# A two-layer hybrid decoder trunk: three more granules of weights split through GpSimd's DMAs, the last pair of MoBA heads in tiles of its own, and branch B in two phases

## The chip, the cores and the metric

The kernel runs on one core of a Trainium2 chip. The metric is the device time of one execution in microseconds, as the median of several runs. The profile quoted is of one execution of the same program.

## The reference

Two layers, each a gated token mixer and a SwiGLU, both with a residual and a LayerNorm behind. SEQ is 256, D_MODEL 1024, everything float32. What the change touches is the end of the mixer:

```python
def hybrid_mixer(x, w_in, w_branch_sb, w_branch_moba, w_out):
    proj = x @ w_in      # q,k,v of 8 stick-breaking heads, q,k,v of 8 MoBA heads, two gates
    ...
    o_sb = stick_breaking_attention(...)
    o_mb = moba_attention(...)           # 256 keys are one block: causal softmax attention
    branch_sb = merge_heads(o_sb) @ w_branch_sb      # [256,512] @ [512,1024]
    branch_mb = merge_heads(o_mb) @ w_branch_moba    # [256,512] @ [512,1024]
    merged = jax.nn.sigmoid(g_sb) * branch_sb + jax.nn.sigmoid(g_mb) * branch_mb
    return merged @ w_out                            # [256,1024] @ [1024,1024]

# per layer
x = layer_norm(alpha * x + hybrid_mixer(x, ...))
x = layer_norm(alpha * x + (silu(x @ w_gate) * (x @ w_up)) @ w_down)
```

## The kernel before

**Three products for one.** Every float32 operand is split into a rounded part `hi` and the rest `lo` (both in the type fp32r), and a product is three matmuls on TensorE (PE): hi by hi, lo by hi, hi by lo. The helper `mm3` issues them, and `mm` records them, so PE's rows all stand on L427.

**Granules.** The weights of a layer are cut into 122 granules of 128x1024 float32 (512 KB). A ring of 10 slots (`NSPLIT`) holds split granules, `whi` and `wlo`; a slot comes free when PE is done with the granule ten before. There are two ways to split a granule. A *hard* one is loaded by SyncE's queue into one of 6 `raw` buffers, cast to `whi` by ScalarE (ACT, L48), and `wlo` = raw - whi is made by VectorE (DVE, L53). A *soft* one (the numbers in `SOFT_IN_LAYER`) needs neither `raw` nor DVE: a DMA issued by GpSimd (POOL) casts it into `whi` on the way, ACT writes -whi into `wlo` (ACTIVATE, L48), and a second DMA of GpSimd adds the weight to `wlo`. GpSimd issues its DMAs in order, each behind what it waits for. Granules 40 to 47 are moved in a pattern of two pieces (L134), the others in one (L137).

Numbers in a layer: 24 to 39 are the gates (PE tiles `pg`), 40 to 43 branch A, which is the stick-breaking side (`pa0` to `pa3`), 44 to 47 branch B, the MoBA side (`pb0` to `pb3`), 48 to 55 the output projection (`pw`), behind it the SwiGLU. In names, `l0` and `l1` are the layers; layer 1's granules are numbered 122 higher.

**MoBA's pairs.** The eight MoBA heads go in four pairs, `mb0` to `mb3`. A pair's softmax weights are turned on DVE and on a way through DRAM (tiles `turn` and `scr`), split into `pp` (a single buffer with a hi and a lo half), and summed with v on PE (`mb_o`). ACT copies the sums of the hi half into `f`, DVE adds the rest, and `f` is split into one 128-row part of `omb_hi` and `omb_lo`, which is step k = p of branch B's contraction. `bounced` makes each pair wait until the one before has been summed, since they share `pp` (the list `summed`).

**Branch B.** `branch(i, 1, ps, ks)` issues the contraction steps `ks` of output granule i, for each of its two 128-column halves: 6 matmuls a step. Before the change these are the steps 0 and 1 of granules 0 to 2 (36 matmuls), then step 2 of granules 0 to 2 (18) and steps 0 and 1 of granule 3 (12), then the rest. `summed_up` multiplies a finished granule by its gate, adds branch A's share (`gate`), and splits it into `m_hi` and `m_lo`, the operands of `pw`.

**Order.** Each engine runs its instructions in the order in which they are recorded. A planner (`Weave`) sets it as the program is built: generators (`split_line`, `bounced` and others) yield the time at which they can go on, by costs written in the program, and are stepped in between the matmuls; `weave.finish(sides)` records all that is left of the named generators first.

## Time and profile before

| | us |
|---|---|
| median of 3 runs | 725.62 (725.59 to 725.67) |
| the profiled execution | 725.78 |
| its span (first to last instruction) | 724.0 |
| PE busy | 710.8 |
| DVE busy | 528.6 |
| ACT busy | 389.8 |
| POOL busy | 34.5 |

The profile's times start at the beginning of the span; the profiled execution's time lies 1.78 us above its span. The stretch of which the prediction speaks, from the end of the gates to the output projection, lies at about 112 to 175 us in layer 0 and at 467 to 530 us in layer 1. Matmuls are pipelined: a row's duration overlaps the next one's, and what a matmul costs is read from start to start.

### The profile page before, as it was taken

What the parts mean: (1) busy time and instruction counts of PE and PEld (TensorE: products, weight loads), DVE (VectorE), ACT (ScalarE), POOL (GpSimd) and SP (SyncE); (2) the same over time, 40 slices, a digit from 0 to 9 for tenths busy, and PEclk for the clock granted to TensorE, in tenths of its full rate; (3) what the DMA queues carried; (4) which work ended last, traced back from release to release, by engine and by line L of the source; (5) the groups of instructions that cost most, each with busy time, mean ns of one, the idle gap of its engine ahead of it and who ended that gap; (6) DMA issues with size and microseconds to landing.
All of it is one profiled execution on the core that took longest, in us unless ns stands there. A gap on an engine that the chain in (4) does not pass through costs nothing.

```text
span 724.0 us, 12718 instructions
## 1 busy us (share of the span) xinstructions
PE 710.8 (98%) x4984; PEld 650.5 (90%) x4984; DVE 528.6 (73%) x790; ACT 389.8 (54%) x581; POOL 34.5 (5%) x48
## 2 busy tenths in 40 slices
PE   8999999999999999999999999999999999999995
PEld 6889899987899999988889889999788999998885
DVE  5999886798886666643688887869989776665416
ACT  5767667654665554442365566775555555454300
POOL 0001110000000000000000111100010000000001
PEclk9999999999999999999999999999999999999999
DMA  8998889776596655476259589795749965663501
GB/s 294 337 342 234 226 214 270 223 247 234 188 333 220 202 183 196 146 293 200 80 163 353 164 218 232 201 297 175 265 136 290 295 217 180 200 202 99 224 1 58
DMA packets 61596, 156.26 MB, mean 216 GB/s; under 512 B 10720, under 2 KB 21984, under 8 KB 61536
## 3 DMA queue, kind: packets, MB, share of 16 engines
q1 hardware_dynamic: 56848, 140.50, 58.2%
q0 software_dynamic: 4544, 14.68, 9.4%
q8 instruction: 39, 0.64, 0.4%
q10 hardware_dynamic: 144, 0.26, 0.1%
q14 instruction: 21, 0.17, 0.1%
HBM read 148.08 MB, written 7.34 MB: 215 GB/s over the span
## 4 chain that ended last, share of the span: by engine, by line
PE 87%; DVE 7%; DMA 3%; issue 2%; ACT 1%; SPq 0%; POOL 0%; POOLq 0%; DVEq 0%; ACTq 0%
PE l1pf L427 14%; PE l0pf L427 14%; PE l0pd L427 8%; PE l0pg L427 6%; PE l1pg L427 5%; PE l1pe L427 4%; PE l1pd L427 4%; PE l1pft L427 3%; PE l1pqk L427 3%; PE l0pqk L427 3%; PE l0pft L427 3%; PE l1pvq L427 3%; DVE wlo L53 3%; PE l1pw L427 2%; PE l0pw L427 2%; PE l1pk L427 2%
## 5 line engine op out<-in xcount | busy, mean ns | idle before, releaser
L53 DVE TENSOR_TENSOR wlo<-raw,whi 128x1024 fp32r<-128x1024 f32 (+1 forms) x234 | 277.5, 1202 | 83.0 <-ACT whi L48 80.1
L48 ACT CAST whi<-raw 128x1024 fp32r<-128x1024 f32 (+1 forms) x233 | 237.6, 1035 | 83.8 <-PE l0pd L427 19.6
L427 PE MATMUL l1pf<-xT_hi,wlo 128*128 128x256 f32 x288 | 79.6, 276 | 0.0
L427 PE MATMUL l1pf<-xT_hi,whi 128*128 128x256 f32 x288 | 79.6, 276 | 0.0
L427 PE MATMUL l1pf<-xT_lo,whi 128*128 128x256 f32 x288 | 79.6, 276 | 0.0
L427 PE MATMUL l0pf<-xT_hi,wlo 128*128 128x256 f32 x288 | 79.5, 276 | 0.0
L427 PE MATMUL l0pf<-xT_hi,whi 128*128 128x256 f32 x288 | 79.5, 276 | 0.0
L427 PE MATMUL l0pf<-xT_lo,whi 128*128 128x256 f32 x288 | 79.5, 276 | 0.0
L427 PEld LDWEIGHTS l1pf<-xT_hi,whi 128*128 128x128 f32 x288 | 54.1, 188 | 0.0
L427 PEld LDWEIGHTS l1pf<-xT_lo,whi 128*128 128x128 f32 x288 | 54.1, 188 | 0.0
L427 PEld LDWEIGHTS l1pf<-xT_hi,wlo 128*128 128x128 f32 x288 | 54.1, 188 | 0.0
L427 PEld LDWEIGHTS l0pf<-xT_hi,whi 128*128 128x128 f32 x288 | 54.1, 188 | 0.0
L427 PEld LDWEIGHTS l0pf<-xT_lo,whi 128*128 128x128 f32 x288 | 54.1, 188 | 0.0
L427 PEld LDWEIGHTS l0pf<-xT_hi,wlo 128*128 128x128 f32 x288 | 54.1, 188 | 0.0
L427 PE MATMUL l0pg<-xT_hi,whi 128*128 128x256 f32 x128 | 35.8, 280 | 0.2 <-DVE l0vmb L53 0.2
L427 PE MATMUL l1pg<-xT_hi,whi 128*128 128x256 f32 x128 | 35.7, 279 | 0.0
L427 PE MATMUL l0pg<-xT_hi,wlo 128*128 128x256 f32 x128 | 35.4, 277 | 0.0
L427 PE MATMUL l0pg<-xT_lo,whi 128*128 128x256 f32 x128 | 35.4, 276 | 0.0
L427 PE MATMUL l1pg<-xT_lo,whi 128*128 128x256 f32 x128 | 35.4, 276 | 0.0
L427 PE MATMUL l1pg<-xT_hi,wlo 128*128 128x256 f32 x128 | 35.4, 276 | 0.0
L427 PE MATMUL l0pd<-whi,l0h_hi 128*128 128x512 f32 x88 | 34.5, 392 | 0.0
L427 PE MATMUL l0pd<-whi,l0h_lo 128*128 128x512 f32 x88 | 34.3, 389 | 0.0
(349 smaller groups left out, 1783.2 us busy)
## 6 DMA issues: line engine op xcount, KB each, us to landing
raw<-in_w_dram SPq DMA_DIRECT2D x226, 512.0 KB, 4.8
whi<-in_w_dram POOLq DMA_DIRECT2D x14, 512.0 KB, 5.0
wlo<-in_w_dram POOLq DMA_DIRECT2D x14, 512.0 KB, 6.5
ln<-in_ln_dram SPq DMA_DIRECT2D x8, 512.0 KB, 6.1
raw<-in_w_dram SPq DMA_DIRECT2D x7, 256.0 KB, 6.1
l0mb_scr<-l0mb_turn SPq DMA_DIRECT2D x4, 384.0 KB, 4.9
l0mb_turn<-l0mb_scr SPq DMA_DIRECT2D x16, 96.0 KB, 6.1
l1mb_scr<-l1mb_turn SPq DMA_DIRECT2D x4, 384.0 KB, 7.1
```

What stands on the lines that cost most here:

```text
L48: f(*args, **kw)
L53: f(*args, **kw)
L427: nc.tensor.matmul(o, a, b, start=start, stop=stop)
```

## The change

Three edits. (1) Granule 40 of each layer becomes hard and 43, 46, 49 and 52 become soft, so that a layer has 10 soft granules instead of 7. (2) The last pair (p = 3) gets two tiles of its own, `w0` and `w1`, for the hi and the lo of its weights, and does not wait for `summed`; since these are two tiles, its sums are eight matmuls of 256 and 128 columns, where they were four of 512 and 256. Of pairs 2 and 3, `f` now lies in the last 256 columns of the `turn` tile. (3) Branch B runs steps 0 and 1 of all four granules first (48 matmuls), then finishes all pairs, then runs steps 2 and 3 together.

```diff
-SOFT_IN_LAYER = (22, 25, 28, 31, 34, 37, 40)
+SOFT_IN_LAYER = (22, 25, 28, 31, 34, 37, 43, 46, 49, 52)
...
     def bounced(name, p, src, there, v, oT, e, f):
         pT, e = yield from bounce_line(name, there, there, src, 6, e)
-        begun.append(name)
-        ...
-        parts = (blocked(pp[:, i].rearrange("p h (k c) -> p (h k) c", c=P)) for i in range(2))
-        e = yield from split_line(*parts, pT, 768, e)
-        yield from both_parts(name, p, v, oT, e, p == NPAIR - 1)
+        if p == NPAIR - 1:
+            ws = [pl.tile([P, 2, 384], F32R, tag="T", name=f"{name}_w{i}") for i, pl in enumerate((work, page0))]
+        else:
+            begun.append(name)
+            mine = len(begun)
+            while len(summed) < mine:
+                yield
+            e = max(e, summed[-1])
+            yield e
+            ws = [pp[:, i] for i in range(2)]
+        e = yield from split_line(*(blocked(x.rearrange("p h (k c) -> p (h k) c", c=P)) for x in ws), pT, 768, e)
+        yield from both_parts(name, p, v, oT, e, ws if p == NPAIR - 1 else None, f)
...
         for h, o in enumerate(os):
             vs = [x[:, p, 2 * h:2 * h + 2, :].rearrange("p r c -> p (r c)") for x in v]
-            mm(o, vs[0], pp[:, :, h, :S], True, False)
-            mm(o[:, :, P:], vs[1], pp[:, :, h, S:], False, True)
+            if ws:
+                for i, w in enumerate(ws):
+                    mm(o[:, i], vs[0], w[:, h, :S], i == 0, False)
+                    mm(o[:, i, P:], vs[1], w[:, h, S:], False, i == 1)
+            else:
+                mm(o, vs[0], pp[:, :, h, :S], True, False)
+                mm(o[:, :, P:], vs[1], pp[:, :, h, S:], False, True)
         e = pe_done()
-        summed.append(e)
+        if not ws:
+            summed.append(e)
...
-            there = unit(f"{name}_turn", [P, 1024])[:, :768]
+            there = unit(f"{name}_turn", [P, 1024])
+            there, f = there[:, :768], there[:, 768:]
...
-        for i in range(3):
-            branch(i, 1, pbs[i], range(2))
-        weave.finish(sides[:-1])
-        for i in range(3):
-            branch(i, 1, pbs[i], range(2, 3))
-        branch(3, 1, pbs[3], range(2))
+        for i in range(4):
+            branch(i, 1, pbs[i], range(2))
         weave.finish(sides)
...
-        branch(0, 1, pbs[0], range(3, 4))
+        branch(0, 1, pbs[0], range(2, 4))
...
         for i in (1, 2):
-            branch(i, 1, pbs[i], range(3, 4))
+            branch(i, 1, pbs[i], range(2, 4))
```

The order on DVE in layer 0, from the end of branch A to the end of branch B. A number behind a name counts the buffers that the program has taken; for `raw46` to `raw50` the first number is the granule. `wlo_99<-raw..` is the split of a hard granule, `mb2_f` and `mb3_f` the additions of the last two pairs, `omb_lo` their splits. Before:

```order
L53 TENSOR_TENSOR wlo_99<-raw46_1477,whi_98 128x1024
L53 TENSOR_TENSOR l0mb2_f_1729<-l0mb2_o0_1718,l0mb2_f_1729 64x256 x2
L53 TENSOR_TENSOR l0mb2_f_1729<-l0mb2_o1_1719,l0mb2_f_1729 64x256 x2
L53 TENSOR_TENSOR pp_168<-l0mb3_turn_1412,pp_168 128x768
L53 TENSOR_TENSOR l0gate3_1455<-l0gate3_1455,l0pa3_1707 128x2x256
L53 TENSOR_TENSOR wlo_99<-raw47_1491,whi_98 128x1024
L53 TENSOR_TENSOR wlo_99<-raw48_1504,whi_98 128x1024
L53 TENSOR_TENSOR l0omb_lo_1018<-l0mb2_f_1729,l0omb_hi_1017 128x256
L53 TENSOR_TENSOR wlo_99<-raw49_1540,whi_98 128x1024
L53 TENSOR_TENSOR l0mb3_f_1803<-l0mb3_o_1791,l0mb3_f_1803 64x256 x4
L53 TENSOR_TENSOR wlo_99<-raw50_1556,whi_98 128x1024
L53 TENSOR_TENSOR l0omb_lo_1018<-l0mb3_f_1803,l0omb_hi_1017 128x256
```

After, at the same place:

```order
L53 TENSOR_TENSOR l0mb3_w1_1708<-l0mb3_turn_1411,l0mb3_w0_1707 128x768
L53 TENSOR_TENSOR wlo_99<-raw47_1476,whi_98 128x1024
L53 TENSOR_TENSOR l0mb2_turn_1374<-l0mb2_o0_1726,l0mb2_turn_1374 64x256 x2
L53 TENSOR_TENSOR l0mb2_turn_1374<-l0mb2_o1_1727,l0mb2_turn_1374 64x256 x2
L53 TENSOR_TENSOR l0gate3_1453<-l0gate3_1453,l0pa3_1714 128x2x256
L53 TENSOR_TENSOR wlo_99<-raw48_1501,whi_98 128x1024
L53 TENSOR_TENSOR l0mb3_turn_1411<-l0mb3_o_1750,l0mb3_turn_1411 64x256 x4
L53 TENSOR_TENSOR l0omb_lo_1018<-l0mb2_turn_1374,l0omb_hi_1017 128x256
L53 TENSOR_TENSOR wlo_99<-raw50_1515,whi_98 128x1024
L53 TENSOR_TENSOR l0omb_lo_1018<-l0mb3_turn_1411,l0omb_hi_1017 128x256
```

The splits of 46 and 49 are gone from this row, and the last pair's weights (`w1`) are split ahead of pair 2's additions. Behind it come the splits of 51 and 53, and 54 between the additions of the first gate (before: 51 alone). Ahead of the last `m_lo` four splits stood in a row (52 to 55), and now that of 55 alone.

The order on ACT in layer 0, around the split of pair 0's weights (`pp`). Before:

```order
L48 CAST whi_98<-raw39_973 128x1024
L48 CAST whi_98<-raw41_1074 128x1024
L48 CAST whi_98<-raw42_1078 128x1024
L48 CAST pp_168<-l0mb0_turn_1197 128x768
L48 CAST whi_98<-raw43_1146 128x1024
```

After:

```order
L48 CAST whi_98<-raw39_973 128x1024
L48 ACTIVATE wlo_99<-whi_98 128x1024
L48 CAST whi_98<-raw40_1074 128x1024
L48 CAST whi_98<-raw41_1078 128x1024
L48 CAST pp_168<-l0mb0_turn_1197 128x768
L48 ACTIVATE l0gate3_1453<-l0pg6_1454 128x512
L48 CAST whi_98<-raw42_1146 128x1024
```

The ACTIVATE is the negation of granule 43, now ahead of the casts of 40 and 41 and of `pp`; it can start when GpSimd's first DMA of 43 has landed.

The order on GpSimd in layer 0, where the last soft granules are issued, as a difference (- before, + after):

```order
 L137 DMA whi<-in_w_dram 128x1024
 L137 DMA wlo<-in_w_dram 128x1024
-L134 DMA whi<-in_w_dram 128x2x512
-L134 DMA wlo<-in_w_dram 128x2x512
+L134 DMA whi<-in_w_dram 128x2x512 x2
+L134 DMA wlo<-in_w_dram 128x2x512 x2
+L137 DMA whi<-in_w_dram 128x1024 x2
+L137 DMA wlo<-in_w_dram 128x1024 x2
 L58 ISA
```

Granule 40's two DMAs are replaced by those of 43 and 46, both casts first, and behind them those of 49 and 52, before GpSimd's own small work (`ISA`) of the LayerNorm.

## The prediction

> **What bounds the kernel now.** I read the page first, then the waits of TensorE (PE), then PE's timeline around each wait.

> ```profile
> span 724.0 us, 12718 instructions
> PE 710.8 (98%) x4984; PEld 650.5 (90%) x4984; DVE 528.6 (73%) x790; ACT 389.8 (54%) x581; POOL 34.5 (5%) x48
> ...
> PE l0pw L427 <- DVE l0m_lo L53: 0.8, 1, 0.8
> PE l1pw L427 <- DVE wlo L53: 0.7, 2, 0.5
> PE l0pb L427 <- DVE l0omb_lo L53: 0.6, 1, 0.6
> PE l0pw L427 <- DVE wlo L53: 0.4, 1, 0.4
> PE l1pb L427 <- DVE l1omb_lo L53: 0.4, 1, 0.4
> ```

> PE is busy for 98% of the span, and no PE work is taken out, so only its idle time can be won. The waits (total us, times, longest) list six of them in the stretch that the change touches: pb and pw, in both layers, all on VectorE (DVE). They sum to 2.9 us. An idle figure understates the loss, because the matmul after a wait also starts late. PE's timeline (start, duration) shows that:

> ```profile
> 150.07 0.28 PE L427 MATMUL l0pb<-l0omb_hi,whi 128*128 128x256 f32 x1
> 150.98 0.39 PE L427 MATMUL l0pb<-l0omb_lo,whi 128*128 128x256 f32 x1 [0.63 <-DVE l0omb_lo L53]
> 151.20 0.28 PE L427 MATMUL l0pb<-l0omb_hi,wlo 128*128 128x256 f32 x1
> ...
> 160.79 0.50 PE L427 MATMUL l0pw<-wlo,l0m_hi 128*128 128x512 f32 x1 [0.45 <-DVE wlo L53]
> ...
> 164.79 0.50 PE L427 MATMUL l0pw<-whi,l0m_lo 128*128 128x512 f32 x1 [0.77 <-DVE l0m_lo L53]
> ...
> 130.98 0.70 PE l0mb_o L427 x4
> 131.68 7.53 PE l0pa L427 x66
> ```

> The last two rows are from the chain that ended last: 66 matmuls of 256 columns in 7.53 us are 0.114 us each. In the first three, two starts that should take 2 x 0.114 take 1.13: 0.90 is lost where the row says 0.63, so 0.27 more. The six waits lose 2.9 + 6 x 0.27 = 4.5 us, 2.6 of it in layer 0. That is the most the change can win.

> **Why DVE is late.** Its timeline in layer 0 (`wlo<-raw,whi` is the split of a granule of weights):

> ```profile
> 143.83 2.35 DVE L53 TENSOR_TENSOR wlo<-raw,whi 128x1024 fp32r<-128x1024 f32 x2
> 146.10 0.42 DVE L53 TENSOR_TENSOR l0omb_lo<-l0mb_f,l0omb_hi 128x256 fp32r<-128x256 f32 x1
> 146.43 1.22 DVE L53 TENSOR_TENSOR wlo<-raw,whi 128x1024 fp32r<-128x1024 f32 x1
> 147.57 1.76 DVE L53 TENSOR_TENSOR l0mb_f<-l0mb_o,l0mb_f 64x256 f32<-64x256 f32 x4
> 149.36 1.23 DVE L53 TENSOR_TENSOR wlo<-raw,whi 128x1024 fp32r<-128x1024 f32 x1
> 150.51 0.42 DVE L53 TENSOR_TENSOR l0omb_lo<-l0mb_f,l0omb_hi 128x256 fp32r<-128x256 f32 x1
> 153.68 0.42 DVE L53 TENSOR_TENSOR l0m_lo<-l0gate,l0m_hi 128x256 fp32r<-128x256 f32 x1
> 156.32 0.69 DVE L53 TENSOR_TENSOR l0m_lo<-l0gate,l0m_hi 128x512 fp32r<-128x512 f32 x1
> 159.51 4.62 DVE L53 TENSOR_TENSOR wlo<-raw,whi 128x1024 fp32r<-128x1024 f32 x4
> 164.06 0.68 DVE L53 TENSOR_TENSOR l0m_lo<-l0gate,l0m_hi 128x512 fp32r<-128x512 f32 x1
> ```

> Between 143.83 and the last pair's `omb_lo` stand four granule splits; from 159.51 four more stand in a row ahead of the last `m_lo`, the one PE waits for at 164.79. DVE runs without a break, so its order is its time here: a split started right behind another costs 4.62/4 = about 1.15.

> **The change, part by part.**

> *Granules 40 to 43, 46, 49, 52.* Three splits per layer go (10 soft ones for 7), and 43 goes soft where 40 did. By the order, 46 and 49 leave the queue ahead of the last `omb_lo`; 52 leaves the four ahead of the last `m_lo`. ScalarE (ACT) trades casts for negations of the same tile, about 1.0 us either way, so I cost that at zero.

> *MoBA steps in two phases.* The last pair's `omb_lo` is read by the 68th matmul of branch B now (36, 18 and 12, then the product of its hi) and by the 53rd after (48, three of step 2, the product of its hi): 15 x 0.114 = 1.7 us earlier. Unstalled it was due at 150.07 + 0.11 = 150.18; it is now due at 150.18 - 1.7 + 0.2 (the longer sums of the last pair, below) = 148.7. DVE came at 150.93; without 46 and 49 it comes 2 x 1.15 = 2.3 earlier: 148.6. In time by 0.1 at best, so the wait of 0.9 goes, but without slack. The first `m_lo` loses 46 and 49 and gains 53 and 54 ahead of it: it stays at 154.1, due at 154.2; the second ends at 157.0, due about 156.95. For the residue of these near ties in both layers I take 0.3, bounds 0 and 1.0 (one wait as large as the largest of now).

> *Output projection.* 52 soft: the wait on `wlo` at 160.79 (0.7 with its tail) goes. The last `m_lo` ended at 164.74; three splits fewer ahead make it 161.3, due at about 162.5: that wait (1.0) goes, with 1.2 to spare. Layer 1:

> ```profile
> 503.29 2.36 DVE L53 TENSOR_TENSOR wlo<-raw,whi 128x1024 fp32r<-128x1024 f32 x2
> 505.57 0.42 DVE L53 TENSOR_TENSOR l1omb_lo<-l1mb_f,l1omb_hi 128x256 fp32r<-128x256 f32 x1
> ```

> Two splits stand directly ahead of the last `omb_lo` there too. By the new order I get 503.1 to 503.6 for it, due at 504.0; the two waits of pw on `wlo` go with 174 soft. So 1.9 us of layer 1 go.

> *The last pair in its own tiles.* Its sums are eight matmuls, four of 256 and four of 128 columns, for four of 512 and 256. By columns alone nothing changes (-0.02 to 0). But the scores show (PE's timeline, pairs on 64 rows):

> ```profile
> 42.69 0.28 PE L559 MATMUL l0sb_s<-l0qkhi,l0qklo 64*128 64x128 f32 x2
> 42.80 0.33 PE L559 MATMUL l0sb_s<-l0qkhi 64*128 64x256 f32 x2
> ```

> A pair of 128 columns takes 0.11 from start to start, as much as 256 columns elsewhere. So I take 8 x 0.114 = 0.91 for 0.70: +0.21 in each layer, +0.42; bounds 0 and 0.42. The split of this pair no longer waits for pair 2's matmuls, which pulls it forward on DVE; but it cannot start before the pair's way through DRAM is over, and that is not shortened.

> *Six more transfers per layer from GpSimd.* A soft granule is a cast into `whi`, a negation by ACT, and an accumulate into `wlo`. Its rows (GpSimd's issues by tile, ns min/median/max; casts to landing, of all and of granule 40's alone; the timelines of GpSimd and ACT; two windows with the DMA share and GB/s at their end; the queues of plain and of GpSimd's transfers):

> ```profile
> L134 POOL DMA_DIRECT2D whi<-in_w_dram x2: 747/750/752, 104.6 to 459.6; - x2
> DMA to landing us min/median/max: 3.6/5.0/9.1
> ...
> L134 POOL DMA_DIRECT2D wlo<-in_w_dram x2: 1183/1190/1198, 114.0 to 470.1; - x2
> ...
> DMA to landing us min/median/max: 8.0/8.0/8.0
> ...
> 104.57 0.75 POOL L134 DMA_DIRECT2D whi<-in_w_dram  x1 [1.04 <-PE l0pg L427]
> 112.62 1.06 ACT L48 ACTIVATE wlo<-whi 128x1024 fp32r<-128x1024 f32 x1 [1.67 <-DMA whi<-in_w_dram]
> 118.51 2.93 ACT L48 CAST whi<-raw 128x1024 fp32r<-128x1024 f32 x3
> 121.34 0.83 ACT L48 CAST pp<-l0mb_turn 128x768 fp32r<-128x768 f32 x1
> ...
> 112.00:152.00 40.00, 39.37 (x336) 38.84 (x336) 30.85 (x45) 26.93 (x39) 1.20 (x1) 1.00 0.82 245
> 475.00:485.00 10.00, 10.00 (x88) 9.92 (x88) 8.79 (x11) 6.99 (x11) 0.00 (x0) 1.00 1.05 346
> q1 hardware_dynamic: 56848, 140.50, 58.2%
> q0 software_dynamic: 4544, 14.68, 9.4%
> ```

> Granule 40's cast, in the two-piece pattern that 43 and 46 have too, was issued at 104.57 when granule 30's slot came free, took 8.0 us, and ACT waited 1.67 for it. 43 waits for granule 33's slot, three granules of 24 matmuls later: 104.57 + 72 x 0.114 = 112.8. With 8.0 to 9.1 us to land it is there at 120.8 to 121.9. By the new order ACT needs it behind the first of the three casts that begin at 118.51, ahead of two more and pair 0's split (121.34). I work the limit back from pair 0's sums on PE, which move six gate matmuls back to 125.6: split 0.95, ACT 0.83, two casts of 0.98, negation 1.06 put it at 120.7. So this one lands on its limit or up to 1.2 us behind, and PE waits in order. The same working for 46 gives 121.5 issued, limit 130.1: 8.6 us. 49, 52 and layer 1 have 6.7 to 11 us, in the plain pattern or with more slack. For all of these I take 0.5, bounds 0 and 2.

> Are the transfers themselves slowed? From the two queue rows a soft transfer occupies the engines for 9.4% x 724 / 28 = 2.4 us, a raw load about 58.2% x 724 x 0.524 / 140.5 = 1.6; six more and three fewer per layer are +9.9 us in some 40: a DMA share of 0.82 becomes 1.07. That reads as full, but by bytes it is 245 + 1.57 MB / 40 us = 284 GB/s, and ten microseconds of layer 1 ran at 346 with a share of 1.05. I take it as room left and no slowing, and leave the slowing to a rival.

> *The sum.* -4.5 + 0.3 + 0.42 + 0.5 = -3.3 on this execution (span 724.0, run 725.78, 0.16 above the median of 725.62): span 720.7, run 722.5, against the median **722.3**.

> **Rivals.** *A, slower: soft transfers come late at ACT.* Place: the negation of 43, then 46, which ACT now takes ahead of the splits of pairs 0 and 2. Each us behind the limit is a us of PE idle at `mb_o`. To be slower by 0.2% (1.45 us, about what a measurement of this kernel can tell) the new waits must reach 3.3 + 1.5 = 4.8 us beyond the 0.5, for instance 2.5 in each layer: a landing of 10.5 to 11.5 us where the longest cast shown took 9.1. With DMA share already 0.82 it is possible: 728. For it speaks ACT's 1.67 of waiting before; against, the 346 GB/s.

> *B, part of the gain: the end of the last pair's way sets DVE, not its splits.* Then pb's waits stay (0.9 + 0.7) and the doubled sums and near ties are paid: -4.5 + 1.6 + 0.4 + 0.3 + 0.5 = -1.7, 724.0. The deadline came 1.7 us nearer, and I have it met by 0.1 to 0.9.

> *C, nothing moves:* DVE fills the place of the three splits with 53 and 54, which the order does put ahead of the first `m_lo`; the waits of pb and pw stay, in other places, at their 4.5 less what the steps' new order wins: about 725.5.

> *D, GpSimd's issues stretch under DVE.* Here they took 747 to 752 and 1183 to 1198 ns in a stretch in which DVE was busy for 30.85 of 40 us; if DVE could hold them up by two of its splits (2.4 us), 43 and 46 of layer 0 would each miss by some 2 us more: -3.3 + 4 = 0.7, 726.3. [...]

> **How the numbers follow.** Forecast, 721 to 723.6: 0.52, since each term has a row but three deadlines are near ties. B, 723.6 to 724.6: 0.20. C: 0.11. D: 0.05, about the same as before. A: 0.08. All near ties fall well (below 721): 0.04. The range reaches from 721.0 over the forecast and B into C, to 725.3. Faster: 0.52 + 0.04 + most of B = 0.75; same: the rest of B, C, D = 0.17; slower 0.08.

> **What would show it.** In the profile after: no pb and pw rows among PE's waits, or rows under 0.3; `mb_o` of eight matmuls in about 0.9 us; ACT's negations waiting for `whi` by under 1 us; a DMA share near 1 in 112 to 152 with casts landing within 9 us; four `wlo` splits fewer at 159.5. Wrong would be a wait of PE on `mb_o` or `pp`, or on `omb_lo` with DVE idle ahead of it.

## The result, and the profile after

| | before | after |
|---|---|---|
| median, us | 725.61 | 733.75 (730.22 to 734.88) |
| ratio to before | | 1.0105 (95%: 1.0069 to 1.0140) |
| profiled execution, us | 725.78 | 730.22 |
| its span, us | 724.0 | 728.4 |

The change makes the kernel 1.05% slower; 722.3 was forecast, and 733.75 lies far outside the range. The profiled execution is the shortest of the four runs; a later profile of a long one is shown below. The page of the kernel after, its first lines and GpSimd's queue (packets, MB, share):

```profile
span 728.4 us, 12741 instructions
PE 713.7 (98%) x4992; PEld 655.5 (90%) x4992; DVE 522.6 (72%) x784; ACT 390.3 (54%) x581; POOL 44.3 (6%) x60
...
q0 software_dynamic: 6784, 20.97, 12.7%
```

DVE has 6 us less to do, as intended, and GpSimd's queue carries 20.97 MB for 14.68. PE's waits after (total us, times, longest):

```profile
PE l0mb_o L427 <- ACT l0mb_w L48: 2.2, 1, 2.2
...
PE l1mb_o L427 <- ACT l1mb_w L48: 1.3, 1, 1.3
PE l1pb L427 <- DVE l1omb_lo L53: 0.8, 1, 0.8
PE l1mb_o L427 <- DVE l1mb_w L53: 0.6, 1, 0.6
PE l0mb_o L427 <- DVE l0mb_w L53: 0.3, 1, 0.3
```

Five of the six waits of before are gone: all of pw, and pb in layer 0. In their place PE waits in both layers for the last pair's sums. The chain that ended last, in layer 0 (start, duration), says what these waited for:

```profile
124.26 9.80 DMA l0mb_turn<-l0mb_scr
...
134.07 8.42 DMA l0mb_turn<-l0mb_scr
...
142.60 0.84 ACT l0mb_w L48
...
143.46 0.97 DVE l0mb_w L53
...
144.47 1.54 PE l0mb_o L427 x6
146.01 1.39 PE l0pa L427 x6
```

Pair 3's last load from DRAM took 8.42 us and landed at 142.5; before the change it landed at 135.9. The four loads of this pair and GpSimd's casts, by tile (the first row is the loads before, the second the loads after, the third the casts after; us to landing, min/median/max, layer 0, issued in 127.5 to 140 and for the casts in 112 to 140):

```profile
DMA to landing us min/median/max: 4.9/5.3/7.2
...
DMA to landing us min/median/max: 8.4/9.0/11.4
...
DMA to landing us min/median/max: 4.5/6.7/11.9
```

Of the 6.6 us, 3.1 lie in the last load's issue (134.1 for 131.0) and 3.5 in its own time to landing (8.4 for 4.9). The issue is late because SyncE holds such loads back until earlier transfers have landed, granules of weights above all: 5.8 us in all between 120 and 145, where it was 3.1 before.

The last row of the chain shows something else: six matmuls of branch A in 1.39 us are 0.23 each, twice the 0.114 of before. The granted clock in windows of 1 us (window, length, busy times, then clock, DMA share, GB/s):

```profile
143.00:144.00 1.00, 0.52 (x2) 0.50 (x2) 0.54 (x1) 1.00 (x2) 0.00 (x0) 0.65 1.13 426
144.00:145.00 1.00, 0.69 (x5) 0.53 (x3) 1.00 (x2) 0.95 (x3) 0.00 (x0) 0.50 0.66 242
149.00:150.00 1.00, 1.00 (x7) 1.00 (x7) 0.96 (x3) 1.00 (x2) 0.37 (x1) 0.50 1.04 320
150.00:151.00 1.00, 1.00 (x10) 1.00 (x10) 0.92 (x4) 0.29 (x2) 0.49 (x1) 0.94 0.80 225
```

Near the end of the 2.2 us without a matmul the clock is halved, and it stays so from about 143.3 to 150.1 (6.8 us), long after work is there again. Where the time went by stage, from the first and last starts of one product of each (before, then after):

```profile
L427 PE MATMUL l0pa<-l0osb_hi,whi x32: 276/276/288, 129.5 to 141.5; 128*128 128x256 f32 x32
L427 PE MATMUL l0pw<-whi,l0m_hi x32: 387/390/477, 154.4 to 178.4; 128*128 128x512 f32 x32
L427 PE MATMUL l0pft<-whi,xT_hi x32: 387/389/486, 179.1 to 201.2; 128*128 128x512 f32 x32
L427 PE MATMUL l1pa<-l1osb_hi,whi x32: 276/276/386, 484.5 to 496.8; 128*128 128x256 f32 x32
L427 PE MATMUL l1pw<-whi,l1m_hi x32: 388/389/477, 509.5 to 532.8; 128*128 128x512 f32 x32
L427 PE MATMUL l1pft<-whi,xT_hi x32: 387/389/479, 533.5 to 556.1; 128*128 128x512 f32 x32
...
L427 PE MATMUL l0pa<-l0osb_hi,whi x32: 276/276/522, 129.4 to 146.6; 128*128 128x256 f32 x32
L427 PE MATMUL l0pw<-whi,l0m_hi x32: 387/389/477, 159.5 to 181.6; 128*128 128x512 f32 x32
L427 PE MATMUL l0pft<-whi,xT_hi x32: 389/389/486, 182.3 to 204.4; 128*128 128x512 f32 x32
L427 PE MATMUL l1pa<-l1osb_hi,whi x32: 276/276/287, 487.6 to 499.6; 128*128 128x256 f32 x32
L427 PE MATMUL l1pw<-whi,l1m_hi x32: 389/389/477, 515.3 to 537.4; 128*128 128x512 f32 x32
L427 PE MATMUL l1pft<-whi,xT_hi x32: 388/389/479, 538.1 to 560.7; 128*128 128x512 f32 x32
```

| from first start to first start, us | before | after | |
|---|---|---|---|
| layer 0, pa to pw (both branches) | 24.9 | 30.1 | +5.2 |
| layer 0, pw to pft | 24.7 | 22.8 | -1.9 |
| layer 1, pa to pw | 25.0 | 27.7 | +2.7 |
| layer 1, pw to pft | 24.0 | 22.8 | -1.2 |

The projection wins 3.1 us and the branches lose 7.9; the rest of the span differs by 0.4. Of layer 0's 5.2 the two waits take 3.0 from start to start, the longer sums 0.2, and the wait on `omb_lo` that went gives 0.9 back. That leaves 2.9 for the halved clock; 2.1 of it are the 20 matmuls of the branches between 145.8 and 150.2, which take 4.4 us where 20 x 0.114 is 2.3.

### The profile page after: what moved, and what is told of

Same layout as the page of the kernel before. It is cut to its first block, busy times and chain, and to the rows that moved or that the text cites. A ratio compares the mean times of both kernels' runs of the same rounds, so it can differ in the third digit from the quotient of the medians.

```text
span 728.4 us, 12741 instructions
## 1 busy us (share of the span) xinstructions
PE 713.7 (98%) x4992; PEld 655.5 (90%) x4992; DVE 522.6 (72%) x784; ACT 390.3 (54%) x581; POOL 44.3 (6%) x60
## 3 DMA queue, kind: packets, MB, share of 16 engines
q0 software_dynamic: 6784, 20.97, 12.7%
## 4 chain that ended last, share of the span: by engine, by line
PE 88%; DMA 6%; DVE 3%; ACT 1%; issue 1%; SPq 0%; POOL 0%; POOLq 0%; DVEq 0%; ACTq 0%
PE l1pf L427 13%; PE l0pf L427 13%; PE l0pd L427 8%; PE l1pg L427 5%; PE l0pg L427 5%; PE l1pe L427 4%; PE l1pd L427 4%; PE l1pft L427 3%; PE l1pqk L427 3%; PE l0pqk L427 3%; PE l0pw L427 3%; PE l1pvq L427 3%; PE l0pft L427 3%; PE l1pw L427 3%; DMA l0mb_turn<-l0mb_scr 3%; DMA l1mb_turn<-l1mb_scr 3%
## 5 line engine op out<-in xcount | busy, mean ns | idle before, releaser
L53 DVE TENSOR_TENSOR wlo<-raw,whi 128x1024 fp32r<-128x1024 f32 (+1 forms) x228 | 270.6, 1202 | 84.7 <-ACT whi L48 81.7
L48 ACT CAST whi<-raw 128x1024 fp32r<-128x1024 f32 (+1 forms) x227 | 232.0, 1035 | 85.1 <-PE l0pd L427 19.6
L427 PE MATMUL l1pf<-xT_hi,whi 128*128 128x256 f32 x288 | 79.6, 276 | 0.0
L427 PE MATMUL l1pf<-xT_hi,wlo 128*128 128x256 f32 x288 | 79.6, 276 | 0.0
L427 PE MATMUL l1pf<-xT_lo,whi 128*128 128x256 f32 x288 | 79.6, 276 | 0.0
L427 PE MATMUL l0pf<-xT_hi,whi 128*128 128x256 f32 x288 | 79.5, 276 | 0.0
L427 PE MATMUL l0pf<-xT_hi,wlo 128*128 128x256 f32 x288 | 79.5, 276 | 0.0
L427 PE MATMUL l0pf<-xT_lo,whi 128*128 128x256 f32 x288 | 79.5, 276 | 0.0
L427 PEld LDWEIGHTS l1pf<-xT_hi,whi 128*128 128x128 f32 x288 | 54.1, 188 | 0.0
L427 PEld LDWEIGHTS l1pf<-xT_lo,whi 128*128 128x128 f32 x288 | 54.1, 188 | 0.0
L427 PEld LDWEIGHTS l1pf<-xT_hi,wlo 128*128 128x128 f32 x288 | 54.1, 188 | 0.0
L427 PEld LDWEIGHTS l0pf<-xT_lo,whi 128*128 128x128 f32 x288 | 54.1, 188 | 0.0
L427 PEld LDWEIGHTS l0pf<-xT_hi,whi 128*128 128x128 f32 x288 | 54.1, 188 | 0.0
L427 PEld LDWEIGHTS l0pf<-xT_hi,wlo 128*128 128x128 f32 x288 | 54.1, 188 | 0.0
L427 PE MATMUL l0pg<-xT_hi,whi 128*128 128x256 f32 x128 | 35.8, 280 | 0.2 <-DVE l0vmb L53 0.2
L427 PE MATMUL l1pg<-xT_hi,whi 128*128 128x256 f32 x128 | 35.7, 279 | 0.0
L427 PE MATMUL l0pg<-xT_hi,wlo 128*128 128x256 f32 x128 | 35.4, 277 | 0.0
L427 PE MATMUL l0pg<-xT_lo,whi 128*128 128x256 f32 x128 | 35.4, 277 | 0.0
L427 PE MATMUL l1pg<-xT_lo,whi 128*128 128x256 f32 x128 | 35.4, 276 | 0.0
L427 PE MATMUL l1pg<-xT_hi,wlo 128*128 128x256 f32 x128 | 35.3, 276 | 0.0
L427 PE MATMUL l0pd<-whi,l0h_hi 128*128 128x512 f32 x88 | 34.5, 391 | 0.0
L427 PE MATMUL l0pd<-wlo,l0h_hi 128*128 128x512 f32 x88 | 34.3, 389 | 0.0
```

Of the source, the lines that this page charges most:

```text
L48: f(*args, **kw)
L53: f(*args, **kw)
L427: nc.tensor.matmul(o, a, b, start=start, stop=stop)
```

## The experiments

Two theories stood at the start. **T1**: GpSimd's additional transfers slow the loads from DRAM that bring back the last pair's turned weights. **T2**: the planner now asks for that pair's sums too early, whatever the transfers do. Each kernel was compared with the kernel before on the same chip.

**The soft granules of before, the rest of the change kept.**

```diff
-SOFT_IN_LAYER = (22, 25, 28, 31, 34, 37, 43, 46, 49, 52)
+SOFT_IN_LAYER = (22, 25, 28, 31, 34, 37, 40)
```

> The changed kernel with the seven soft granules of before; the last pair's own tiles and the two phases stay. T1 (the soft transfers hold up the last pair's loads from DRAM): the last load of pair 3 lands near 136 us in layer 0 and 491 in layer 1 as before, PE does not wait on mb_o by more than 0.3, the granted clock stays at 1.00 from 140 to 150, and the time is 724 to 726.5 (granules 46 and 49 are back on DVE, so waits on omb_lo and in pw remain, and the eight sums cost 0.4). T2 (the new order asks for the last pair's sums too early, whatever the transfers do): PE still waits on mb_o by over 1 us in layer 0 and the time is 728 or more.

Measured 726.61 us, ratio 1.0012 (1.0003 to 1.0021). The last load landed at 136.0 and 491.3, and no wait on `mb_o` is left, so T2 falls: early asking alone does not make PE wait there. Its waits:

```profile
PE l0pb L427 <- DVE l0omb_lo L53: 2.0, 1, 2.0
PE l1pb L427 <- DVE l1omb_lo L53: 1.8, 1, 1.8
```

Own tiles and two phases alone win nothing: they bring the deadline of `omb_lo` forward while DVE still has 46 and 49 ahead of it, and 0.6 and 0.4 become 2.0 and 1.8. From 140 to 150 the clock stayed at 1.00, as expected, but behind the wait of 2.0, which ended at 150.3, it was halved from about 151.3 to 154.7.

**The ten soft granules alone**, in the kernel before (the same line, the other way round).

> The kernel before with the ten soft granules and nothing else. T1: the last load of pair 3 lands 5 us or more later than before in both layers (141 or later, 497 or later). Pair 3's sums stand some 8 us further back on PE here than in the changed kernel, so PE waits little on mb_o, and the lateness shows as a wait on omb_lo in pb of 1 to 3 us: 726 to 730. T2: the loads land within 2 us of before, and the time is 724 or less, since the three DVE splits are gone and nothing is asked for early.

Measured 728.31 us, ratio 1.0041 (1.0027 to 1.0056): slower without any other part of the change. The last load landed at 142.6 and 501.0, as T1 has it. The wait is in pb:

```profile
PE l1pb L427 <- ACT l1omb_hi L48: 2.7, 2, 1.7
PE l0pb L427 <- ACT l0omb_hi L48: 1.6, 1, 1.6
PE l0pb L427 <- DVE l0omb_lo L53: 0.8, 1, 0.8
```

In this profile the clock stayed at 1.00. By the medians on this chip, the ten soft granules alone cost 2.9 us and the two other edits alone 1.2, but in the changed kernel all three cost 8.1. Some 4 us thus arise only where late loads meet sums that are asked for early.

**Half the bytes.** The transfers of 43, 46, 49 and 52 by GpSimd move half of their columns; the order on every engine is that of the changed kernel.

```diff
+            if start == self.nc.gpsimd.dma_start:
+                start(dst.rearrange("p (c n) -> p c n", c=2)[:, :, :256],
+                      self.w[g:g + 2, :, b * 512:b * 512 + 256].rearrange("c p n -> p c n"), **kw)
+                return
...
+        elif start == self.nc.gpsimd.dma_start and g % NG_LAYER >= 40:
+            start(dst[:, :512], self.w[ORDER.get(g, g), :, :512], **kw)
```

> The changed kernel in which GpSimd's transfers of granules 43, 46, 49 and 52 move half of their columns (the other half of these granules is left as it is in the ring, so the output is another one); every instruction, wait and the order on all engines stay. T1 by bytes: pair 3's last load lands at 137 to 139 in layer 0 (142.5 in the changed kernel, 135.9 before), PE's waits on mb_o come to under 1 us for both layers together, the clock stays up, and the time is 722 to 725. T1 by number of transfers (each one holds the queues for its own time, whatever its size): landing stays at 141 or later and the time at 729 or more. T2: no change, 730 to 735.

Measured 721.63 us, ratio 0.9946 (0.9931 to 0.9961), 0.4 under the range. The last load landed at 139.7, 0.7 later than expected, and at 492.6. That is T1, by bytes: GpSimd's queue has as many packets as in the changed kernel (6784), with 16.78 MB for 20.97. Its row, and what is left of the waits in the branches and the projection:

```profile
q0 software_dynamic: 6784, 16.78, 11.0%
...
PE l0pb L433 <- DVE l0omb_lo L53: 0.8, 1, 0.8
PE l0mb_o L433 <- DVE l0mb_w L53: 0.2, 1, 0.2
```

This is the kernel that the prediction described (722.3), with nothing changed but the size of eight pairs of transfers.

**Casts or accumulates.** The same edit, once for the casts alone and once for the accumulates alone (`and not kw`, `and kw` in the two conditions).

> The changed kernel in which only the casts of 43, 46, 49 and 52 move half their columns (the rest of whi stays as the ring had it, so the output is another one); the accumulates move all. Pair 3's last load landed at 142.5 in layer 0 with all bytes and at 139.7 with half of both. If casts and accumulates hold up the loads alike per transfer, the landing is about 141, PE waits 1 to 2 us on mb_o in layer 0 and the time is 724 to 729. If the casts carry it, it lands near 139.7 and the time is 721 to 723.5.

> The changed kernel in which only the accumulates of 43, 46, 49 and 52 move half their columns (the output is another one). If alike per transfer: landing about 141, 724 to 729. If the accumulates carry it (in the kernel before one took 6.5 us to land where a cast took 5.0): landing near 139.7 and 721 to 723.5.

Measured 725.15 us, 0.9994 (0.9978 to 1.0010), and 725.07 us, 0.9996 (0.9985 to 1.0007). By the medians each edit gives back about 8 us, and both together 12, so neither kind carries it alone. Landing in layer 0 was 140.2 and 141.7, but these two cannot be set against each other: the first profile is of one of the shortest of ten runs (723.11), the second of the longest of ten (727.16).

**The sums asked for later.**

```diff
         if ws:
+            e += 4.0
             yield e + MARGIN
```

> The changed kernel in which the planner takes pair 3's weights to be there 4 us later, so that its sums stand 36 matmuls (4.1 us) further back on PE in layer 0 and 39 in layer 1; the transfers are as in the changed kernel. If what PE lost was only the place of the sums, the wait on mb_o goes in layer 0 (it was 2.5 us), the clock stays at 1.00, and the time is 723 to 725. If the pair's whole chain is late, the wait comes back on omb_lo in pb, 1 to 3 us in each layer: 725 to 729, with a clock that falls again where a wait passes about 2 us.

Measured 737.43 us, ratio 1.0167 (1.0147 to 1.0187): worse than either outcome that was expected. The wait on the last pair's sums goes; the kernel's waits in pb, beside one of 1.3 us on `omb_hi` in layer 1:

```profile
PE l1pb L427 <- DVE l1gate L53: 3.1, 1, 3.1
PE l0pb L427 <- ACT l0omb_hi L48: 2.9, 1, 2.9
PE l0pb L427 <- DVE l0gate L53: 1.4, 1, 1.4
```

The 4 us stand on the planner's clock and moved other work too (the two waits on `gate` are new), so this run does not show what the place alone costs. The granted clock was halved for some 3.4 us in layer 0 and 13.7 in layer 1.

**PE kept busy.** Beside the late loads, the halved clock is the second cause to test.

```diff
+            if ws and h == 0:
+                for _ in range(24):
+                    nc.tensor.matmul(o[:, 0], vs[0], v[0][:, 0].rearrange("p r c -> p (r c)"), start=True, stop=True)
```

> The changed kernel with 24 matmuls of 256 columns (2.7 us) put on PE just ahead of the last pair's sums, in each layer; they write into the place of the sums, which then overwrite it, and wait for nothing that is late. PE gets 5.4 us of work more. If the idle time itself is all that the wait costs, the fillers take the place of 2.4 and 1.4 us of waiting and add what is over, 0.3 and 1.3 us: 1 to 2 us above the changed kernel, 732 to 736. If the idle time makes the granted clock fall (0.50 from 145 to 150 us in the changed kernel), and that costs what PE's matmuls lose there (about 2.4 us in layer 0 of the profiled run, more in longer runs), the clock stays at 1.00 from 140 to 155 and from 500 to 510, and the time is 727 to 729 and spreads less: PE works more and the kernel is faster.

Measured 729.26 us, ratio 1.0059 (1.0037 to 1.0081), against 1.0105 (1.0069 to 1.0140) and, in the next run, 1.0098 (1.0073 to 1.0123) without the fillers. The clock reads 1.00 from 130 to 155 and from 495 to 515, and the last loads land as late as before (142.4 and 499.9). The intervals overlap a little, but PE does 5.4 us more work and the median is 4 us lower. It lies 0.3 above the range of 727 to 729, and the runs spread no less than before (728.1 to 732.0). The waits that remain:

```profile
PE l0pb L427 <- DVE l0omb_lo L53: 0.8, 1, 0.8
PE l1pb L427 <- DVE l1omb_lo L53: 0.7, 1, 0.7
```

**The changed kernel again**, for a profile of a longer run.

> The changed kernel once more, on the chip of these runs, for a second profile of it: its first four runs went from 730.2 to 734.9. If the spread comes from the clock that falls after PE's wait on mb_o, a longer run shows more or longer stretches under 1.00, in layer 1 too, with landings within a microsecond of the first profile's (142.5 and 500.8); if it comes from the transfers, the landings differ by 2 us or more.

Measured 733.09 us, ratio 1.0098 (1.0073 to 1.0123); the profiled execution took 734.73. The loads landed at 143.1 and 503.6, so 2.7 us later in layer 1 than in the first profile. The wait there grew from 1.3 to 3.5, and now the clock was halved in layer 1 as well, from about 505.1 to 511.9 (the granted clock stands third from the end):

```profile
PE l1mb_o L427 <- ACT l1mb_w L48: 3.5, 1, 3.5
PE l0mb_o L427 <- ACT l0mb_w L48: 3.2, 1, 3.2
...
505.00:506.00 1.00, 0.50 (x3) 0.50 (x3) 1.00 (x2) 0.96 (x3) 0.00 (x0) 0.53 0.87 180
511.00:512.00 1.00, 1.00 (x6) 1.00 (x6) 0.94 (x3) 0.57 (x1) 0.00 (x0) 0.56 1.02 283
```

From the first start of pa to that of pw the branches take 30.8 us in layer 0 and 31.9 in layer 1, 5.8 and 6.9 more than before; less the projection's 3.1 and 0.8 elsewhere, this makes the 8.9 by which this span is the longer one. Both causes that were set against each other are in it: a landing that varies decides whether a wait is long enough for the clock.

**Soft granules that stay clear of the loads**, in the kernel before: 52 alone, 49 and 52, 50 and 53.

```diff
-SOFT_IN_LAYER = (22, 25, 28, 31, 34, 37, 40)
+SOFT_IN_LAYER = (22, 25, 28, 31, 34, 37, 40, 52)
```

> The kernel before with one soft granule more, 52: its cast goes out at about 138 us, behind the landing of the last pair's loads (135.9 before), so T1 expects these to land as before (within 0.5 us), the waits on omb_lo in pb to stay (0.6 and 0.4), and those in pw to go but for a rest under 0.4 each (2.65 us with their tails in both layers): 723 to 724. If any further soft granule in this stretch costs what it wins, the time stays at 725 to 726.

> The kernel before with 49 and 52 soft. 49's cast goes out at about 130 us, right among the last pair's loads (127.7 to 135.9). T1 by bytes: one cast of 0.5 MB there moves the landing by 1 to 3 us, about half of what three did in the changed kernel; it costs nothing on mb_o, since pair 3's sums stand 5 us later than in the changed kernel, and some on omb_lo if the pair's split is late. 722 to 724.5. If the accumulates, not the casts, slow the loads, the landing stays within 0.5 us of before.

> The kernel before with two soft granules more, 50 and 53, whose casts go out at about 133 and 142 us. 50's split stood directly ahead of the last omb_lo on DVE, so the wait there (0.6 and 0.4) falls by up to 1.15 us. T1: 50's cast goes out as the last pair's loads are on their way (131 to 135.9), which moves their landing by 0 to 2 us, still ahead of need, since pair 3's sums stand in pb1 (146 us). The waits in pb and pw go but for rests: 721.5 to 723.5.

With 52 alone: 721.77 us, ratio 0.9949 (0.9934 to 0.9964), better than both kernels. Its cast goes out at 138.5, behind the last load (135.7), and of the six waits the two of pb are left. It is 1.2 under the range. Of the 4.1 us by which the profile's span is shorter, 3.1 lie in the projection; the other 1.0 lies in stages that the edit does not touch, and why is not shown. The two waits:

```profile
PE l0pb L427 <- DVE l0omb_lo L53: 0.7, 1, 0.7
PE l1pb L427 <- DVE l1omb_lo L53: 0.4, 1, 0.4
```

With 49 too: 722.30 us, 0.9962 (0.9951 to 0.9973); 49's cast at 129.2 moves the landing to 139.1, PE waits 1.0 us for the last pair's weights in layer 1, where no wait was expected, and one granule more wins nothing. With 50 and 53: 724.52 us, 0.9992 (0.9969 to 1.0015), where a win was expected. The landing moved to 138.1 only, but 53's cast came late for ACT: its negation waited 4.70 us for it, and `omb_hi` stands behind it (ACT's timeline):

```profile
152.45 1.06 ACT L48 ACTIVATE wlo<-whi 128x1024 fp32r<-128x1024 f32 x1 [4.70 <-DMA whi<-in_w_dram]
153.42 0.39 ACT L48 CAST l0omb_hi<-l0mb_f 128x256 fp32r<-128x256 f32 x1
```

PE waited 3.3 us for that `omb_hi`, and behind the wait the clock was halved for 3.4 us. This is the prediction's rival A in its own form, in another kernel and with another granule.

**52 soft, and splits with a shorter lead.**

```diff
-LEAD = 4
+LEAD = 3
```

> The kernel before with 52 soft as well, and the planner's lead for splits cut from 4 granules to 3, so that 50's split stands behind the last omb_lo on DVE (51's behind the gate sums). No transfer moves into the last pair's loads. The rests in pb (0.84 and 0.57 us with their tails) go: 720 to 721.5 against 721.8 for 52 alone. If splits that come later elsewhere make PE wait for them (in pw, or in the SwiGLU), the time is 723 or more.

Measured 722.71 us, ratio 0.9957 (0.9940 to 0.9973), 0.9 above 52 alone in the medians, and the intervals overlap. The waits of pb go, as expected, and others take their place:

```profile
PE l0pw L427 <- DVE wlo L53: 1.0, 1, 1.0
PE l0pw L427 <- ACT whi L48: 0.3, 1, 0.3
PE l1pft L427 <- DVE wlo L53: 0.3, 1, 0.3
```

## Why the prediction was wrong

- **The step that failed** is the term "six more transfers per layer": 0.5 us, bounds 0 and 2, from "room left and no slowing". It came to some 12 us: 733.75 with all the bytes, 721.63 with half of those of four granules. The share of 0.82 that becomes 1.07 was in the text; I set it aside because 284 GB/s lies under the 346 of another window. But a mean of bytes says nothing of how long one load takes beside others. The loads' median went from 5.3 to 9.0 us, one issued behind the landing of another, so the last came 6.6 us later. I had looked for the late transfer at the negations of 43 and 46, ahead of pairs 0 and 2, and left the last pair's loads at their old time ("not shortened"). The sign that the prediction named for being wrong, PE waiting on `mb_o`, is the one that came.
- **That a wait costs its idle time plus 0.27** failed as well. It held for waits up to 0.8 us (0.79 on `omb_lo` in layer 1 after the change cost 1.05). After 2.0 us and more the granted clock was halved for 3.4 us or about twice or four times that, and each such stretch cost PE up to half its length: 2.9 us in layer 0 of the first profile and, worked out in the same way, about 3 in layer 1 of the second.
- **Rival A** had the right resource and sign, 728 and a chance of 0.08. Its point of decision (a cast of 10.5 us or more) was reached by casts of up to 11.9; its place was another. **Rival B** had the right place, the end of the last pair's way, but at its old time (724.0).
- **The gain** was right in the projection: 1.7 us were forecast in layer 0 and 1.2 in layer 1, and from first to first start it is 1.9 and 1.2 shorter after the change. In pb it came in one layer alone. In the kernel with half the bytes, where the waits of pw are gone too and the time is 721.63, `omb_lo` of layer 0 was "in time by 0.1" and there came 0.8 late, behind sums that themselves waited 0.2; layer 1 met it.
- **The eight sums** cost what the rows of the attention scores said, or a little less. PE's timeline in the kernel with the soft granules of before:

```profile
498.27 1.04 PE L427 MATMUL l1mb_o<-l1mb_w,l1vmb 128*128 128x256 f32 x8
499.14 0.33 PE L427 MATMUL l1pb<-l1omb_hi,whi 128*128 128x256 f32 x1
```

0.87 us from start to start for a forecast of 0.91, against 0.70 for the four.
- **43's cast** was forecast on its limit or up to 1.2 us late. It landed at 117.2 in the first profile, 4.5 us after its issue, and PE never waited at pair 0.
- **Rival D** stayed out. That DVE could hold GpSimd's issues up by 2.4 us was the author's estimate, and no run showed it. The loads that were late are issued by SyncE, and halving the bytes alone removed nearly all of their wait. GpSimd's issues in the two stretches took 0.57 to 1.24 us after the change, and the longest took 1.20 before.

## What to carry to other kernels

The DMAs that relieved one engine here were paid for by the loads in flight beside them, whose median to landing went from 5.3 to 9.0 us. Ask which load on the critical way is issued in the same ten microseconds, and move the new traffic behind its landing: one more soft granule, issued 2.8 us after the last load, won 0.5%; three more, with casts among the loads, lost 1% with the rest of the change and 0.4% alone. On TensorE, treat one wait of about 2 us as costlier than several short ones that lie apart: behind the 2.2 us in layer 0 came 2.9 more at a halved clock, and behind the six waits of before, of 0.8 at most, the clock stayed at 1.00.
